# Reordering the last pair of quads in a Strassen-like QKV projection

## The chip, the cores and the metric

The kernel runs on one core of a Trainium2 chip. The metric is the device time of one execution in microseconds; the median of several runs is given. A core has a matrix engine (PE), a vector engine (VectorE, DVE in the profile), a scalar engine (ScalarE, ACT), GpSimd (POOL) and a queue engine (SyncE, SP) that here only issues transfers. All transfers of the core share 16 DMA engines.

## The reference

```python
x:     (16, 512, 768) float32      # 8192 rows of 768
w_qkv: (768, 2304)    float32
qkv = np.matmul(x, w_qkv)
q, k, v = qkv[..., :768], qkv[..., 768:1536], qkv[..., 1536:]
return np.stack([q, k, v], axis=0).astype(np.float32)     # (3, 16, 512, 768)
```

So it is one product of 8192x768 by 768x2304, whose columns are cut into three outputs.

## The kernel before

**Tiling.** The 8192 rows are taken as 32 pairs of 128-row tiles (`NP` = 32). The 2304 columns are two groups of 1024 (`q` = 0 and 1, at columns 0 and 1280) and a remainder of 256 columns between them (`REM`, at column 1024). One pair of row tiles by one column group is a *quad*: a 2x2 arrangement of output blocks c11, c12, c21 and c22, each 128x512, held in one SBUF tile `u.o`.

**Seven products.** A quad is not computed with eight block products but with seven, in the manner of Strassen-Winograd, out of sums of blocks of x (made by GpSimd in `sums_x`) and sums of blocks of w (made once by `sum_w`). `do(u, n)` issues product n (three matmuls of 128x128 by 128x512, in `product`, line 258) and the instruction that takes it out of PSUM. The products of a quad accumulate into three PSUM banks:

- bank `u.x`: product 1, read by ScalarE into c11 (`evacuate`, line 267); product 6 on top of it, read by ScalarE into c12 (line 286); product 7 on top of that, added by VectorE to c22 (line 295); product 4 on top of that, read by ScalarE into c21 (line 301).
- bank `u.y`: product 5, read by ScalarE into c22 (line 291, in the last pair of row tiles); product 3 on top of it, added by VectorE to c12 (line 304).
- bank `u.z`: product 2, added by VectorE to c11 (line 280).

So products 1, 6, 7 and 4 stand in a fixed order, and each of the last three can only start when the one before it has been read out of the bank; the same holds for 5 and 3. There are eight banks in all, handed out in turn by `bank()`.

**The remainder.** `rem_row(p, r, ps)` computes the 256 remaining columns of row tile r of pair p with six bf16 matmuls (line 321). In the last pair `rem_stored(p, r)` does this for one row tile, copies the result out of PSUM in two halves of 128 columns (ScalarE, line 423, and VectorE, line 424) and stores 128 KB from ScalarE's queue (line 426).

**Order.** The schedule is written by hand: each engine executes its instructions in the order in which the program issues them, and the framework only puts in semaphore waits where data or buffers demand it. Over the steady part of the kernel two quads of a pair run interleaved (`summed`, `plain`). The last pair of row tiles is done by `last(a, b)`, where a and b are its two quads. There each block is stored on its own as soon as it is complete (`store_cols`, 256 KB, line 416) from SyncE's queue, except one that goes from ScalarE's. After the last store has landed, the program closes (its waits stand under line 700).

Of the kernel before, what the change touches and what calls it, by code (L numbers as in the profile page):

```python
# [10 lines left out]
def kernel(  # L11
# [20 lines left out]
    nc = tc.nc  # L32
# [10 lines left out]
    CB = 512  # L43
    REM = N3 - 4 * CB
# [5 lines left out]
    ident = mybir.ActivationFunctionType.Identity  # L50
# [189 lines left out]
    def quad(p, q, pool=o_pool, tag="o"):  # L240
        u = Quad()
        u.p, u.q = p, q
        u.o = pool.tile([P, 2, 2 * CB], fp32, name="o", tag=tag)
        u.x = u.y = u.z = None
        return u

    def product(u, n, ps, start):
        t1, t2, t3, t4 = ts[u.q]
        if n <= 2:
            h = (n - 1) * KH  # L250
            lhs = [xb[u.p][:, h + j, :P] for j in range(KH)]
            rhs = [b1[u.q][:, h + j, :] for j in range(KH)]
        else:
            k, t = {3: (4, b22[u.q][:]), 4: (0, t4), 5: (1, t1), 6: (2, t2), 7: (3, t3)}[n]
            lhs = [sr[u.p][:, k, j, :] for j in range(KH)]
            rhs = [t[:, j, :] for j in range(KH)]
        for j in range(KH):
            nc.tensor.matmul(  # L258
                ps[:], lhs[j], rhs[j],
                start=(start and j == 0), stop=(j == KH - 1), skip_group_check=True,  # L260
            )

    def bank():
        return ps_pool.tile([P, CB], fp32, name="ps")

    def evacuate(u):
        nc.scalar.activation(u.o[:, 0, :CB], u.x[:], ident)

    def do(u, n, out=True):
        c11, c12 = u.o[:, 0, :CB], u.o[:, 0, CB:]  # L270
        c21, c22 = u.o[:, 1, :CB], u.o[:, 1, CB:]
        if n == 1:
            u.x = bank()
            product(u, 1, u.x, True)
            if out:
                evacuate(u)
        elif n == 2:
            u.z = bank()
            product(u, 2, u.z, True)
            nc.vector.tensor_tensor(c11, c11, u.z[:], op=add)  # L280
        elif n == 6:
            first = u.x is None
            if first:
                u.x = bank()
            product(u, 6, u.x, first)
            nc.scalar.activation(c12, u.x[:], ident)  # L286
        elif n == 5:
            u.y = bank()
            product(u, 5, u.y, True)
            if u.p == NP - 1:  # L290
                nc.scalar.activation(c22, u.y[:], ident)
        elif n == 7:
            product(u, 7, u.x, False)
            if u.p == NP - 1:
                nc.vector.tensor_tensor(c22, c22, u.x[:], op=add)
            else:
                nc.scalar.activation(c22, u.x[:], ident)  # L297
                nc.vector.tensor_tensor(c22, c22, u.y[:], op=add)  # L298
        elif n == 4:
            product(u, 4, u.x, False)  # L300
            nc.scalar.activation(c21, u.x[:], ident)  # L301
        elif n == 3:
            product(u, 3, u.y, False)
            nc.vector.tensor_tensor(c12, c12, u.y[:], op=add)  # L304
# [14 lines left out]
    def rem_row(p, r, ps):  # L319
        for j in range(KT):  # L320
            nc.tensor.matmul(  # L321
                ps, xb[p][:, j, r * P:(r + 1) * P], w_rem[j // KH][:, j % KH, :],
                start=(j == 0), stop=(j == KT - 1), skip_group_check=True,
            )
# [77 lines left out]
    def store_cols(u, r, lo, hi, eng):  # L402

        c = Q_OFF[u.q] + lo
        n = hi - lo
        row = (2 * u.p + r) * P
        src = u.o[:, r, lo:hi]
        left = (c // H + 1) * H - c
        if left >= n:
            dst = out_flat[c // H, row:row + P, c % H:c % H + n]  # L410
        else:
            assert 2 * left == n
            first = out_flat[c // H, row:row + P, c % H:H]
            dst = bass.AP(first.tensor, first.offset, [[H, P], [M * H - H + left, 2], [1, left]])
            src = src.rearrange("m (s n) -> m s n", s=2)
        eng.dma_start(dst, src)

    def rem_stored(p, r):
        ps = bank()
        rem_row(p, r, ps[:, :REM])  # L420
        o = or_pool.tile([P, 2, REM], fp32, name="orem")
        half = REM // 2
        nc.scalar.activation(o[:, 0, :half], ps[:, :half], ident)  # L423
        nc.vector.tensor_copy(out=o[:, 0, half:], in_=ps[:, half:REM])  # L424
        row = (2 * p + r) * P
        nc.scalar.dma_start(out_flat[1, row:row + P, R_OFF - H:R_OFF - H + REM], o[:, 0, :])

    def last(a, b):

        do(a, 1)  # L430
        do(b, 1)
        rem_stored(a.p, 0)
        for u in (a, b):
            do(u, 2)
            store_cols(u, 0, 0, CB, nc.sync)
        do(a, 6)
        do(b, 6)
        for u in (a, b):
            do(u, 5)
            do(u, 7)  # L440
            store_cols(u, 1, CB, 2 * CB, nc.sync)
        for u in (a, b):
            do(u, 4)
            store_cols(u, 1, 0, CB, nc.scalar if u is a else nc.sync)
            do(u, 3)
            store_cols(u, 0, CB, 2 * CB, nc.sync)
        rem_stored(a.p, 1)


# [130 lines left out]
    u = quad(2, 0)  # L580
# [72 lines left out]
    for p in range(ND + 3, NP - 1, 2):  # L653
# [14 lines left out]
        a, b = quad(p, 0), quad(p, 1)  # L668
# [3 lines left out]
        plain(a, b, c, d, early, lambda: rem(c.p)()(), final)  # L672
        summed(c, d, {} if final else {0: lambda: transpose(p + 3, 2, 0)}, "parts" if final else True)
    last(quad(NP - 1, 0), quad(NP - 1, 1))


# [28 lines left out]
```

## Time and profile before

| what | value |
|---|---|
| median of 3 runs | 359.17 us (358.98 to 359.32) |
| the profiled execution's own time | 358.81 us |
| span in its profile (first to last instruction) | 357.0 us |
| PE busy | 350.6 us, 98% of the span |
| VectorE, ScalarE, GpSimd busy | 264.4, 185.0, 177.3 us |
| granted clock of PE | 1.00 of full speed |
| last pair begins on PE at | 342.93 us |
| last matmul ends, last store is issued | 353.68, 354.35 us |

The execution's own time is 1.8 us longer than the span, which counts from the first to the last instruction of the program. Times in the views are microseconds from the span's start. In a line such as `352.36 0.60 ACT L301 ... x1 [0.76 <-PE ps L258]` the columns are the start, the length, the engine, the line of the kernel, the operation with its operands and shapes, the number of instructions, and in brackets how long the engine was idle before and which engine, tile and line ended that. PEld is the weight load of the matrix engine, which can overlap its matmuls; a matmul's length includes its way through the array, so that matmuls in a row start closer together than they are long.

### The profile page before, as it was taken

The numbers are of one execution on the slowest core, as the hardware profiler recorded it, in microseconds if no ns is written. First come the engines' busy times: TensorE is split into PE (matmuls) and PEld (weight loads), VectorE is DVE, ScalarE is ACT, GpSimd is POOL, SyncE is SP. The second block draws the span as 40 slices with busy tenths as digits, with TensorE's granted clock in tenths as the row PEclk, the third lists the DMA queues.
The fourth block names the chain that finished last, engine by engine and source line by source line (L and its number), as shares of the span: only waits on it lengthen the run. The fifth ranks groups of instructions, "written<-read, shape, count | busy, mean of one in ns | idle before, by whom it ended". The sixth has DMA issues, their size and how long they took to land.

```text
span 357.0 us, 5315 instructions
## 1 busy us (share of the span) xinstructions
PE 350.6 (98%) x1757; PEld 252.1 (71%) x1776; DVE 264.4 (74%) x310; ACT 185.0 (52%) x317; POOL 177.3 (50%) x184
## 2 busy tenths in 40 slices
PE   7999999999999999999999999999999999999996
PEld 3474677768677686877768677686877768677674
DVE  3789876796877869777695877869777695876743
ACT  4587754545454553645545454553645545454553
POOL 0031773376566453665535566353665535566320
PEclk9999999999999999999999999999999999999999
DMA  7997999999999898998979899698999979887497
GB/s 296 380 353 238 325 378 340 373 317 348 308 311 340 257 361 206 347 266 285 361 197 385 227 342 307 209 402 213 347 263 307 331 196 392 225 303 280 155 380 260
DMA packets 82075, 108.10 MB, mean 303 GB/s; under 512 B 4992, under 2 KB 62080, under 8 KB 82048
## 3 DMA queue, kind: packets, MB, share of 16 engines
q1 hardware_dynamic: 75088, 102.52, 85.7%
q10 hardware_dynamic: 6960, 5.24, 5.5%
q8 instruction: 14, 0.23, 0.3%
q14 instruction: 13, 0.11, 0.1%
HBM read 32.24 MB, written 75.50 MB: 302 GB/s over the span
## 4 chain that ended last, share of the span: by engine, by line
PE 74%; POOL 15%; DVE 6%; issue 3%; DMA 2%; ACT 0%; SPq 0%
PE ps L258 56%; PE ps L321 12%; PE ps L496 6%; DVE xf L155 6%; POOL xb L205 5%; POOL s L226 3%; POOL s L225 3%; POOL s L227 3%; DMA xin<-in_x_dram 2%; PE ps L185 0%; DVE o L304 0%; ACT xc L166 0%; SPq L162 0%; DVE orem L424 0%; ACT orem L423 0%
## 5 line engine op out<-in xcount | busy, mean ns | idle before, releaser
L258 PE MATMUL ps<-t,s 128*128 128x512 f32 x720 | 177.9, 395 | 0.0
L258 PEld LDWEIGHTS ps<-t,s 128*128 128x128 f32 x720 | 135.1, 188 | 29.5
L155 DVE STREAM_TRANSPOSE xf<-xin 128x768 f32<-128x768 f32 (+1 forms) x45 | 93.3, 2075 | 4.3 <-DMA xin<-in_x_dram 4.3
L258 PE MATMUL ps<-b,xb 128*128 128x512 bf16 x343 | 81.6, 379 | 1.1
L298 DVE TENSOR_TENSOR o<-o,ps 128x512 f32<-128x512 f32 x56 | 38.5, 688 | 50.7 <-ACT o L297 50.0
L205 POOL CAST xb<-xf 128x1536 bf16<-128x1536 f32 x28 | 41.1, 1467 | 56.9 <-DVE xf L155 54.8
L225 POOL TENSOR_TENSOR s<-xf 128x384 fp32r<-128x384 f32 x29 | 31.0, 1068 | 72.9 <-DVE xf L155 71.1
L258 PEld LDWEIGHTS <-xb 128*128 128x128 bf16 x360 | 33.9, 98 | 36.7 <-issue 3.9
L304 DVE TENSOR_TENSOR o<-o,ps 128x512 f32<-128x512 f32 x60 | 41.1, 687 | 20.5 <-PE ps L258 19.4
L297 ACT ACTIVATE o<-ps 128x512 f32<-128x512 f32 x56 | 33.5, 598 | 42.1 <-PE ps L258 42.1
L258 PE MATMUL ps<-b,s 128*128 128x512 f32 x180 | 50.6, 389 | 0.0
L301 ACT ACTIVATE o<-ps 128x512 f32<-128x512 f32 x60 | 35.9, 598 | 25.2 <-PE ps L258 22.8
L378 DVE TENSOR_TENSOR o<-o,ps 128x512 f32<-128x512 f32 x78 | 47.8, 680 | 0.0
L321 PE MATMUL ps<-w_rem,xb 128*128 128x256 bf16 x384 | 47.4, 273 | 0.0
L286 ACT ACTIVATE o<-ps 128x512 f32<-128x512 f32 x60 | 35.9, 599 | 19.4 <-PE ps L258 14.0
L321 PEld LDWEIGHTS <-xb 128*128 128x128 bf16 x384 | 37.3, 98 | 11.5 <-issue 0.5
L335 ACT ACTIVATE orem<-ps 128x512 f32<-128x512 f32 x31 | 18.5, 598 | 48.3 <-PE ps L321 34.0
L258 PEld LDWEIGHTS ps<-b,s 128*128 128x128 f32 x180 | 33.8, 188 | 7.0
L226 POOL TENSOR_TENSOR s<-s,xf 128x384 fp32r<-128x384 f32 x29 | 29.5, 1018 | 2.3
L227 POOL TENSOR_TENSOR s<-xf 128x384 fp32r<-128x384 f32 x29 | 29.4, 1015 | 0.0
L229 POOL TENSOR_TENSOR s<-xf,s 128x384 fp32r<-128x384 f32 x29 | 29.2, 1008 | 0.0
L382 ACT ACTIVATE o<-ps 128x512 f32<-128x512 f32 x26 | 15.5, 598 | 17.9 <-PE ps L258 17.3
(49 smaller groups left out, 161.2 us busy)
## 6 DMA issues: line engine op xcount, KB each, us to landing
out_dram<-o SPq DMA_DIRECT2D x60, 768.0 KB, 4.6
out_dram<-o SPq DMA_DIRECT2D x75, 256.0 KB, 3.8
xin<-in_x_dram SPq DMA_DIRECT2D x88, 192.0 KB, 5.6
out_dram<-orem SPq DMA_DIRECT2D x31, 256.0 KB, 2.2
xin<-in_x_dram ACTq DMA_DIRECT2D x24, 192.0 KB, 4.4
st<-in_w_qkv_dram SPq DMA_DIRECT2D x5, 768.0 KB, 7.9
xin<-in_x_dram SPq DMA_DIRECT2D x2, 768.0 KB, 4.9
st<-in_w_qkv_dram SPq DMA_DIRECT2D x6, 256.0 KB, 6.0
```

Source lines behind the costliest of these rows:

```text
L155: nc.vector.transpose(turned[:, g:g + n], rows[:, g:g + n])
L205: nc.gpsimd.tensor_copy(out=xb[p][:], in_=xf[p][:])
L225: 1: lambda g: g.tensor_tensor(s[:, 1], a21, a22, op=add),
L226: 2: lambda g: g.tensor_tensor(s[:, 2], s[:, 1], a11, op=sub),
L227: 3: lambda g: g.tensor_tensor(s[:, 3], a11, a21, op=sub),
L258: nc.tensor.matmul(ps[:], lhs[j], rhs[j], start=(start and j == 0), stop=(j == KH - 1), skip_group_check=True,)
L286: nc.scalar.activation(c12, u.x[:], ident)
L298: nc.vector.tensor_tensor(c22, c22, u.y[:], op=add)
L301: nc.scalar.activation(c21, u.x[:], ident)
L304: nc.vector.tensor_tensor(c12, c12, u.y[:], op=add)
L321: nc.tensor.matmul(ps, xb[p][:, j, r * P:(r + 1) * P], w_rem[j // KH][:, j % KH, :], start=(j == 0), stop=(j == KT - 1), skip_group_check= ...
L378: dve.tensor_tensor(c, c, u.z[:], op=add)
```

## The change

`last` runs the same products and remainders in another order, and `rem_stored` copies a remainder with one ScalarE instruction of 256 columns instead of two halves on two engines. In the new order the first remainder leaves its place behind product 1 of the second quad and stands behind the second quad's product 7. The first quad's products 7, 4 and 3 are issued before the second quad's 7, 4 and 3. Product 4's store of the first quad goes from SyncE's queue instead of ScalarE's.

```diff
         ps = bank()
         rem_row(p, r, ps[:, :REM])
         o = or_pool.tile([P, 2, REM], fp32, name="orem")
-        half = REM // 2
-        nc.scalar.activation(o[:, 0, :half], ps[:, :half], ident)
-        nc.vector.tensor_copy(out=o[:, 0, half:], in_=ps[:, half:REM])
+        nc.scalar.activation(o[:, 0, :], ps[:, :REM], ident)
         row = (2 * p + r) * P
         nc.scalar.dma_start(out_flat[1, row:row + P, R_OFF - H:R_OFF - H + REM], o[:, 0, :])

         do(a, 1)
         do(b, 1)
-        rem_stored(a.p, 0)
         for u in (a, b):
             do(u, 2)
             store_cols(u, 0, 0, CB, nc.sync)
-        do(a, 6)
-        do(b, 6)
-        for u in (a, b):
-            do(u, 5)
-            do(u, 7)
-            store_cols(u, 1, CB, 2 * CB, nc.sync)
-        for u in (a, b):
-            do(u, 4)
-            store_cols(u, 1, 0, CB, nc.scalar if u is a else nc.sync)
-            do(u, 3)
-            store_cols(u, 0, CB, 2 * CB, nc.sync)
+        for u, n in ((a, 6), (a, 5), (a, 7), (b, 6), (b, 5)):
+            do(u, n)
+        store_cols(a, 1, CB, 2 * CB, nc.sync)
+        do(a, 4)
+        store_cols(a, 1, 0, CB, nc.sync)
+        do(a, 3)
+        store_cols(a, 0, CB, 2 * CB, nc.sync)
+        do(b, 7)
+        store_cols(b, 1, CB, 2 * CB, nc.sync)
+        rem_stored(a.p, 0)
+        do(b, 4)
+        store_cols(b, 1, 0, CB, nc.sync)
+        do(b, 3)
+        store_cols(b, 0, CB, 2 * CB, nc.sync)
         rem_stored(a.p, 1)
```

The products of the last pair on PE, in order (1a is product 1 of the first quad, R0 the first remainder):

```
before: 1a 1b R0 2a 2b 6a 6b 5a 7a 5b 7b 4a 3a 4b 3b R1
after:  1a 1b 2a 2b 6a 5a 7a 6b 5b 4a 3a 7b R0 4b 3b R1
```

## The prediction, made before the changed kernel ran

> **What bounds the kernel now.** I read the chain of waits over the last 14 us first, because the change touches only the last pair of quads. Its columns are start, length and what ran.
>
> ```profile
> 343.00 1.24 PE ps L258 x5
> 344.24 0.66 PE ps L321 x6
> 344.90 8.11 PE ps L258 x36
> 353.01 0.69 PE ps L321 x6
> 353.69 0.02 issue
> 353.71 0.29 ACT orem L423
> 354.00 0.02 issue
> 354.02 0.29 DVE orem L424
> ```
>
> The matrix engine (PE) runs its products end to end without one wait; from 342.93 its row of work is the path. Then come the two half copies of the last remainder, the VectorE half strictly behind the ScalarE half, the store issued at 354.35, its landing, and the close of the program at 357.0. So there are two ways to move the end: a hole in PE's row (every ns of it counts), or a shorter way from PE's last matmul to the last landing.
>
> The second view is the timeline of the same stretch (start, length, engine, line, operation, operands; in brackets the idle time before it and what ended it). From it I take the unit prices.
>
> ```profile
> 350.39 0.69 DVE L295 TENSOR_TENSOR o<-o,ps 128x512 f32<-128x512 f32 x1 [0.67 <-PE ps L258]
> 350.80 0.84 PE L258 MATMUL ps<-b,s 128*128 128x512 f32 x3
> 351.26 0.64 PEld L258 LDWEIGHTS ps<-t,s 128*128 128x128 f32 x3
> 351.49 0.84 PE L258 MATMUL ps<-t,s 128*128 128x512 f32 x3
> 352.17 0.84 PE L258 MATMUL ps<-b,s 128*128 128x512 f32 x3
> 352.36 0.60 ACT L301 ACTIVATE o<-ps 128x512 f32<-128x512 f32 x1 [0.76 <-PE ps L258]
> 352.85 0.83 PE L321 MATMUL ps<-w_rem,xb 128*128 128x256 bf16 x6
> 353.05 0.69 DVE L304 TENSOR_TENSOR o<-o,ps 128x512 f32<-128x512 f32 x1 [0.67 <-PE ps L258]
> 353.71 0.28 ACT L423 ACTIVATE orem<-ps 128x128 f32<-128x128 f32 x1 [0.75 <-PE ps L321]
> 354.02 0.29 DVE L424 COPY orem<-ps 128x128 f32<-128x128 f32 x1 [0.29 <-ACT orem L423]
> 354.35 0.34 ACTq L426 DMA_DIRECT2D out_dram<-orem  x1
> ```
>
> Call the products 1a to 7a of the first quad and 1b to 7b of the second, R0 and R1 the remainders. The rows 351.49 (4b) and 352.17 (3b) give a pitch of 0.68 us a product. 4b starts at 351.49 and ScalarE reads its bank at 352.36: a product's bank is read by ScalarE 0.87 after its start, and free again 0.60 later, at +1.47. 7b stands two products ahead of 3a (350.80), so it starts at 349.44; VectorE's add reads it at 350.39, which is +0.95, and frees the bank 0.69 later, at +1.64. A remainder takes 0.66 of PE's row (the chain's second line).
>
> The third view is the table of windows (length, busy time of each engine, granted clock, DMA share, GB/s).
>
> ```profile
> 349.50:351.90 2.40, 2.40 (x12) 2.01 (x11) 1.12 (x3) 1.20 (x2) 0.00 (x0) 1.00 0.39 137
> 351.90:355.50 3.60, 1.78 (x11) 1.07 (x10) 1.45 (x3) 0.87 (x2) 0.00 (x0) 1.00 1.02 378
> ```
>
> The DMA engines first lie mostly idle, then are full to the end: five stores of 256 KB and one of 128 KB come within 4 us.
>
> **The change part by part.** Orders on PE, before and after:
> before: 1a 1b R0 2a 2b 6a 6b 5a 7a 5b 7b 4a 3a 4b 3b R1
> after: 1a 1b 2a 2b 6a 5a 7a 6b 5b 4a 3a 7b R0 4b 3b R1
> The work of PE is the same. What matters is the distance between products on one bank: 1, 6, 7 and 4 of a quad accumulate into bank x, and each must wait until the product before it has been read out; 5 and 3 share bank y.
>
> *Distances that stay harmless.* 1a to 6a: 1b, 2a, 2b lie between, 6a is due 2.7 after 1a and the bank is free at 1.47. 7a to 4a: 6b and 5b lie between, due 2.04, free 1.64, as before. 6b to 7b, 5a to 3a and 5b to 3b have three products or more between. R0 takes a fresh bank. Cost 0, covered by those products; without them each would cost what the next two cost.
>
> *6a to 7a.* Before, 6b and 5a lay between (due 2.04); now only 5a does, so 7a is due at 2 x 0.68 = 1.36, while ScalarE has read 6a only at 1.47. A hole of 0.11 plus the restart r of PE after a release.
>
> *7b to 4b.* Before, 4a and 3a lay between; now R0 does: 4b is due at 0.68 + 0.66 = 1.34, and VectorE's add ends at 1.64. A hole of 0.30 plus r. VectorE is free in time: an add without a second wait starts 0.88 after its product (352.17 to 353.05), so 3a's, one product earlier, ends at 0.88 - 0.68 + 0.69 = 0.89 after 7b's start, ahead of the 0.95.
>
> *The restart r.* After the ramp the kernel shows no hole on PE, so r is bounded by rows of the start-up and of the steady stream. There PE waited for a ScalarE cast:
>
> ```profile
> 6.93 0.52 ACT L166 ACTIVATE xc<-xin 128x384 bf16<-128x384 f32 x1 [1.02 <-DMA xin<-in_x_dram]
> 7.51 0.67 PE L185 MATMUL ps<-eye,xc 128*128 128x128 bf16 x7 [0.58 <-ACT xc L166]
> ```
>
> The cast ended at 7.45, PE's first matmul stands at 7.51: r = 0.06, with bf16 weights. In the stream an f32 weight load at 351.26 precedes its matmul at 351.49 by 0.23; with the 0.06 and a separate wait of PE's sequencer (0.05 in the view of line 258) r is 0.34 at most. I take 0.17, nearer the low end, since in the stream most of the 0.23 is the load standing behind a running matmul, but an f32 load (0.19) is longer than a bf16 one (0.10). The holes are then 0.28 and 0.47, together 0.75; with r = 0.06, 0.53; with r = 0.34, 1.09. [...]
>
> *Who is queued behind.* While PE waits for 4b, 3b and R1 stand behind it, and so does everything to the end: the holes are paid in full.
>
> *The tail.* One ScalarE copy of 128x256 replaces two half copies in a row. ScalarE takes 0.28 for 128 columns and 0.60 for 512, so 256 cost 0.28 + 0.32/3 = 0.39. Before, the copies ended at 354.31, 0.60 after 353.71; now at 0.39: the last store is issued 0.22 earlier behind R1. It landed 1.8 us after issue (the view of line 426). From below: 3b's store (issued 353.76, landed 2.1 later) and R1's share the DMA engines, 128 KB at 378 GB/s are 0.35 us, and if R1's data queue behind 3b's the 0.22 is lost: gain 0. From above: the stores ahead are thinned (R0's 128 KB stands where a 256 KB store stood, and the hole before 4b adds a pause), so both may land with no queue; then 3b's store, landing 2.0 after issue (the least in the view of line 416), is the floor, R1's landing at 0.42 earlier. I take 0.22.
>
> *Moves without a price.* 4a's store goes from ScalarE's queue to SP's: SP's issues take 0.34 to 0.6 each and its stores become ready 0.6 or more apart. R0's copy (0.39) and its store's issue (0.38) now stand on ScalarE's queue behind 4a's read and ahead of 4b's; a remainder is read 0.86 after its start (352.85 to 353.71), so R0's copy runs from 0.68 + 0.86 = 1.54 to 1.93 after 7b's start and the issue ends near 2.35; 4b starts at 1.34 + 0.47 = 1.81 and is read at 2.68: covered by 4b itself. VectorE loses its half copies and the 1.59 it waited for the first; nothing waited for that.
>
> *Sum.* +0.75 - 0.22 = +0.53 on the profiled execution: 358.81 becomes 359.34, its span 357.0 becomes 357.5. That execution stands 0.36 under the median of 359.17, which becomes 359.70. The bounds are 0.53 - 0.42 = +0.11 and 1.09 - 0 = +1.09. A measurement of this kernel can tell about 0.2%, 0.72 us, from no change.
>
> **Rivals.**
> *The holes are dear (slower).* Place: 7a and 4b. If r is near 0.3 on f32 weights and the DMA queue swallows the tail's 0.22, the sum is 0.41 + 0.60 - 0.1 = +0.9: 360.1. With my tail it decides from r = 0.27 on. For it: f32 loads are twice as long as the row behind 0.06. Against it: that row.
> *No hole (a gain).* If the weights for 7a and 4b are ready and releases arrive earlier than the readers' rows say, only the tail is left: -0.22, 358.95; over 0.72 of gain would need more than the 0.42 the tail has. Against it: the order on PE is the written one, and the readers' lengths are fixed within 0.01.
> [...]
>
> **How the numbers follow.** The forecast of two holes of moderate size has 0.60, dear holes 0.30, no hole 0.05, the clock 0.02, and 0.03 is left for a gain over 0.2%. So faster 0.03, same 0.65, slower 0.32. The forecast's own range is 359.3 to 359.9; with the dear holes it reaches 360.4, and with no hole down to 359.0.
>
> **What would show it.** Right: PE idle of about 0.3 ahead of 7a, ended by ScalarE's L286, and about 0.45 ahead of 4b, ended by VectorE's L295; R1 starting near 353.6; a single L422 copy near 0.39; the close 4.6 us after 3b's start (now 4.83). Wrong: PE's row unbroken, or holes over 0.5 each; the last landing still tied to 3b's; a granted clock under 1.00 before the end.

## The result and the profile after

The changed kernel takes 359.76 us (median of 11 runs, 359.65 to 360.33) against 359.00 us before: a ratio of 1.0021, 95% interval 1.0013 to 1.0029. That is 0.75 us more (0.5 to 1.0), slower, and just on the bound that the prediction gave for what a measurement can tell ("about 0.2%, 0.72 us"). The profiled execution took 359.65 us, with a span of 357.9 against 357.0.

The chain that ended last, in order of time, in the changed kernel (start, length, what ran):

```profile
346.96 0.09 issue
347.05 3.68 PE ps L258 x15
350.73 0.02 issue
350.75 0.69 DVE o L304
351.44 0.01 DVEq L295
351.46 0.04 issue
351.50 0.70 DVE o L295
352.20 0.04 issue
352.25 1.66 PE ps L258 x6
353.91 0.68 PE ps L321 x6
354.59 0.02 issue
354.61 0.38 ACT orem L422
```

Before, this was one unbroken row of PE. Now it breaks twice. At 346.96 PE waits before 7a, and from 350.75 to 352.25 the chain leaves PE: it runs through VectorE's adds of 3a (line 304) and 7b (line 295), and PE only comes back when the second has freed bank x of the second quad. The add of 3a stands in the chain because 7b's add follows it on VectorE without a pause, but it did not hold 7b's add up: that began 0.94 after 7b's start, and 0.95 after it in the kernel before, where VectorE had stood idle for 0.67. The timeline has the same two places, with the idle time and its releaser in brackets (rows chosen from the stretch):

```profile
346.30 0.60 ACT L286 ACTIVATE o<-ps 128x512 f32<-128x512 f32 x1 [1.35 <-PE ps L258]
347.02 2.60 PEld L258 LDWEIGHTS ps<-t,s 128*128 128x128 f32 x12 [0.50 <-issue]
350.56 0.84 PE L258 MATMUL ps<-t,s 128*128 128x512 f32 x3
351.24 0.83 PE L321 MATMUL ps<-w_rem,xb 128*128 128x256 bf16 x6
351.50 0.69 DVE L295 TENSOR_TENSOR o<-o,ps 128x512 f32<-128x512 f32 x1
352.25 0.53 PEld L258 LDWEIGHTS ps<-t,s 128*128 128x128 f32 x3 [0.46 <-DVE o L295]
352.25 0.97 PE L258 MATMUL ps<-t,s 128*128 128x512 f32 x3 [0.18 <-DVE o L295]
353.05 0.86 PE L258 MATMUL ps<-b,s 128*128 128x512 f32 x3
354.61 0.38 ACT L422 ACTIVATE orem<-ps 128x256 f32<-128x256 f32 x1 [0.77 <-PE ps L321]
355.03 0.37 ACTq L424 DMA_DIRECT2D out_dram<-orem  x1
```

How to read a hole here: PE's bracket shows only 0.18 us, because a matmul's row (0.39 to 0.40 us in the stream) is longer than the distance to the next one's start (0.227), so that the row before a hole still covers part of the idle time. The true size is in the starts of single matmuls: the last of 5a, the second of 7a, the last of R0 and the second of 4b.

```profile
346.56 0.40 PE L258 MATMUL ps<-t,s 128*128 128x512 f32 x1
347.35 0.39 PE L258 MATMUL ps<-t,s 128*128 128x512 f32 x1
351.80 0.27 PE L321 MATMUL ps<-w_rem,xb 128*128 128x256 bf16 x1
352.58 0.40 PE L258 MATMUL ps<-t,s 128*128 128x512 f32 x1
```

The first two start 0.79 apart, and two pitches of the stream (the distance between the starts of matmuls in a row, 0.227) are 0.45: a hole of 0.34. The other two start 0.787 apart, where without a hole (in the kernel "fillboth" below) it is 0.344: a hole of 0.44.

The windows of the changed kernel around its holes and its tail (length, busy time of the engines, clock, DMA share, GB/s):

```profile
350.50:351.50 1.00, 1.00 (x7) 0.64 (x7) 0.69 (x1) 0.17 (x1) 0.00 (x0) 1.00 0.06 20
351.50:354.20 2.70, 2.52 (x17) 1.72 (x15) 0.94 (x2) 0.98 (x2) 0.00 (x0) 1.00 0.92 340
354.20:354.70 0.50, 0.38 (x4) 0.10 (x1) 0.43 (x1) 0.09 (x1) 0.00 (x0) 1.00 0.00 0
354.70:356.70 2.00, 0.00 (x0) 0.00 (x0) 0.00 (x0) 0.30 (x1) 0.00 (x0) 1.00 0.90 328
```

The queue of stores did empty ahead of the last ones (no byte moved from 354.2 to 354.7), as the prediction had it; but after it, from 354.7 to 356.7, the DMA engines are 0.90 busy again.

For the comparison with the experiments below, every time in this table is counted from the start of the last matmul ahead of the pair (342.54 in the profile before, 342.57 after), since the executions differ by up to 0.7 us in what comes earlier. The starts and landings are read from each kernel's trace; the ratio is of the time to the time of the kernel before.

| kernel | 3b starts | last store issued | 3b's store landed | last store landed | end | ratio (95% interval) |
|---|---|---|---|---|---|---|
| before | 9.62 | 11.80 | 13.30 | 13.64 | 14.47 | 1 |
| changed | 10.48 | 12.46 | 14.12 | 14.45 | 15.29 | 1.0021 (1.0013 to 1.0029) |
| fill7 | 10.18 | 12.15 | 13.81 | 14.14 | 14.98 | 1.0013 (1.0004 to 1.0022) |
| fill4 | 10.03 | 12.01 | 13.72 | 14.07 | 14.97 | 1.0013 (1.0004 to 1.0021) |
| fillboth | 9.71 | 11.69 | 13.39 | 13.72 | 14.62 | 1.0001 (0.9992 to 1.0010) |
| copyonly | 9.62 | 11.58 | 13.29 | 13.64 | 14.47 | 1.0000 (0.9991 to 1.0009) |
| split | 10.48 | 12.68 | 14.11 | 14.44 | 15.28 | 1.0023 (1.0014 to 1.0032) |
| no3b | 9.62 | 11.58 | none | 13.26 | 14.16 | 0.9992 (0.9983 to 1.0001) |
| r0end | 9.00 | 11.86 | 12.68 | 13.56 | 14.40 | 0.9998 (0.9989 to 1.0006) |
| r0endsp | 9.00 | 11.62 | 12.70 | 13.36 | 14.33 | 0.9994 (0.9985 to 1.0003) |

By this count the changed kernel ends 0.82 us later: 3b starts 0.86 later, and the way from 3b's start to the end is 4.81 instead of 4.85.

The last two columns do not always lie equally far apart. When the last store has landed, SyncE still has to find that out: at the close it checks the semaphores of the stores one after the other, in the order of its instructions (in the kernel before the last three of these rows stand at 355.22, 355.86 and 356.20, each 0.02 behind a landing). In six of the ten kernels the last store is checked last, one check follows its landing, and the end comes 0.84 after it. In fill4, fillboth and no3b two checks follow it and the end comes 0.90 after it; in r0endsp three, and 0.97. So a difference of 0.06 between two ends can be one check more, and the landings are the cleaner measure of the stores.

### The profile page after: what moved, and what is told of

It reads as the page before. It is cut to its first block, busy times and chain, and to the rows that moved or that the text cites. A ratio compares the mean times of both kernels' runs of the same rounds, so it can differ in the third digit from the quotient of the medians.

```text
span 357.9 us, 5332 instructions
## 1 busy us (share of the span) xinstructions
PE 352.6 (99%) x1776; PEld 252.0 (70%) x1776; DVE 263.2 (74%) x308; ACT 185.5 (52%) x317; POOL 177.8 (50%) x184
## 4 chain that ended last, share of the span: by engine, by line
PE 97%; DMA 2%; DVE 0%; ACT 0%; SPq 0%; issue 0%; DVEq 0%
PE ps L258 79%; PE ps L321 12%; PE ps L496 6%; DMA xin<-in_x_dram 2%; PE ps L185 0%; DVE o L295 0%; DVE o L304 0%; ACT xc L166 0%; SPq L162 0%; ACT orem L422 0%; DVEq L295 0%
## 5 line engine op out<-in xcount | busy, mean ns | idle before, releaser
L258 PE MATMUL ps<-b,xb 128*128 128x512 bf16 x360 | 85.2, 379 | 0.0
L225 POOL TENSOR_TENSOR s<-xf 128x384 fp32r<-128x384 f32 x29 | 29.5, 1017 | 72.3 <-DVE xf L155 70.6
L227 POOL TENSOR_TENSOR s<-xf 128x384 fp32r<-128x384 f32 x29 | 29.5, 1016 | 0.0
```

What stands on the lines that cost most here:

```text
L225: 1: lambda g: g.tensor_tensor(s[:, 1], a21, a22, op=add),
L258: nc.tensor.matmul(ps[:], lhs[j], rhs[j], start=(start and j == 0), stop=(j == KH - 1), skip_group_check=True,)
```

## The experiments

Theory one: the time is in the two holes. Its first rival: they only move idle time about, and the loss is in the new order of the stores or the copy. A second question is why the single copy gave nothing: whether the last landing follows its issue, or 3b's store. In the excerpts of code, some lines are left out (...), and loops are written out where a line moves.

**fill7**: one product moved into the first hole.

```diff
-        do(b, 2)
-        store_cols(b, 0, 0, CB, nc.sync)
         do(a, 6)
         do(a, 5)
+        do(b, 2)
+        store_cols(b, 0, 0, CB, nc.sync)
         do(a, 7)
```

> The changed kernel with 2b moved to between 5a and 7a, so that 7a is due 2.04 us after 6a's start again. Theory one (the time is in the two holes of the matrix engine, 0.34 ahead of 7a and 0.44 ahead of 4b): the first hole goes, 4b's stays at 0.44; 3b starts about 0.34 earlier than in the changed kernel (near 352.7 us), span near 357.5, time about 0.4 us over the kernel before. Rival (the loss sits in the new order of stores and in the single copy, and the holes only move idle time that was there): span stays near 357.9, 0.75 us over the kernel before.

Its chain:

```profile
344.92 5.71 PE ps L258 x25
...
351.40 0.70 DVE o L295
352.10 0.04 issue
352.14 1.67 PE ps L258 x6
```

The break before 7a is gone (PE runs from 344.92 through it), the one before 4b is as it was. 3b starts 0.31 earlier than in the changed kernel and the end comes 0.31 earlier: the hole of 0.34, less 0.03. The time agrees at 1.0013, 0.5 us over the kernel before, though its interval overlaps that of the changed kernel; the trace carries the verdict.

**fill4**: one product moved into the second hole.

```diff
-        do(a, 3)
-        store_cols(a, 0, CB, 2 * CB, nc.sync)
         do(b, 7)
+        do(a, 3)
         store_cols(b, 1, CB, 2 * CB, nc.sync)
+        store_cols(a, 0, CB, 2 * CB, nc.sync)
         rem_stored(a.p, 0)
```

> The changed kernel with 3a moved to between 7b and the first remainder, so that 4b is due about 2.0 us after 7b's start again. Theory one: 4b's hole of 0.44 goes, 7a's stays at 0.34; 3b starts near 352.6 us, span near 357.4, time about 0.35 us over the kernel before. Rival (stores and copy): span near 357.9.

Its chain:

```profile
347.29 0.09 issue
347.38 4.34 PE ps L258 x18
351.73 0.67 PE ps L321 x6
352.40 1.40 PE ps L258 x6
```

Now the wait before 7a is alone; from R0 (351.73) to 4b there is none, and VectorE is no longer in the chain. 3b starts 0.46 earlier, as much as the hole; the end only 0.32 earlier, since the tail is 0.13 longer again (4.94 from 3b's start to the end, against 4.81). Of that, 0.06 is the second check at the close. The other 0.07 lies ahead of the last landing, in the stores: 4b's and 3b's are issued 0.65 apart instead of 0.79, and 3b's takes 2.08 to land instead of 2.03. That the closer issues are the reason was not tried separately.

**fillboth**: both moves.

> Both moves together on the changed kernel. Theory one: no hole, 3b starts within 0.1 us of the kernel before (352.2 us); the tail after 3b is 0.0 to 0.1 us shorter than before, so span 356.9 to 357.1 and a time within 0.2 us of the kernel before. If the landing of the last store follows its issue by a fixed 1.8 us: 0.2 us faster than the kernel before, span 356.8. Rival (stores and copy): 0.5 us or more over the kernel before.

```profile
344.81 6.38 PE ps L258 x28
351.19 0.67 PE ps L321 x6
351.86 1.40 PE ps L258 x6
353.25 0.68 PE ps L321 x6
```

The chain is PE alone again, and the time is that of the kernel before (1.0001). So the two holes carry the loss, and the rival falls: it asked for 0.5 us or more here. The trace still ends 0.15 later than before, where 0.0 to 0.1 earlier was expected: 3b starts 0.09 late without any hole, and the tail is 0.06 longer. The 0.06 is the second check at the close: from 3b's start to the last landing it is 4.01, as in the kernel before. The order without its holes brings nothing.

**copyonly**: the kernel before with the single copy.

```diff
-        half = REM // 2
-        nc.scalar.activation(o[:, 0, :half], ps[:, :half], ident)
-        nc.vector.tensor_copy(out=o[:, 0, half:], in_=ps[:, half:REM])
+        nc.scalar.activation(o[:, 0, :], ps[:, :REM], ident)
```

> The kernel before with only the single ScalarE copy of 256 columns in place of the two halves. Theory one (the last store's data stand behind the store of 3b in the DMA engines): the last store is issued 0.22 us earlier but lands 0 to 0.06 us earlier, 0.33 to 0.35 us behind 3b's as before; span 356.9 to 357.0, no change in time. Rival (landing follows issue by a fixed 1.8 us): it lands 0.22 us earlier, span 356.8.

Its timeline and then the waits of SyncE's queue at the end (who waited for what: sum, times, longest; line 698 is the close of the program here):

```profile
354.32 0.38 ACT L422 ACTIVATE orem<-ps 128x256 f32<-128x256 f32 x1 [0.75 <-PE ps L321]
354.37 0.34 SPq L416 DMA_DIRECT2D out_dram<-o  x1
354.74 0.34 ACTq L424 DMA_DIRECT2D out_dram<-orem  x1
```

```profile
SPq L698 <- DMA out_dram<-o: 1.6, 3, 0.6
SPq L698 <- DMA out_dram<-orem: 0.3, 1, 0.3
```

The store is issued 0.37 behind 3b's store, where it had been 0.59; that is the 0.22 that the copy saves. It lands at 13.64, to the hundredth where it landed before: its way from issue to landing went from 1.83 to 2.05. In both kernels it lands 0.34 behind 3b's store, the 0.3 in the second line of the waits, and 128 KB at 395 GB/s, which the DMA engines moved from 354.5 to 355.5 in the kernel before, are 0.33 us.

**split**: the changed kernel with the two half copies put back (the edit above, reversed).

> The changed kernel's order with the two half copies put back (only the copy undone). Theory (the copy is worth nothing because the last landing is tied to 3b's): holes as in the changed kernel, the last store issued 0.22 us later, landing within 0.06 us of the changed kernel's, counted from the last pair's start; time 0.6 to 0.9 us over the kernel before. Rival (landing follows issue): 0.2 us later than the changed kernel, about 1.0 us over the kernel before.

```profile
355.16 0.29 DVE L424 COPY orem<-ps 128x128 f32<-128x128 f32 x1 [0.29 <-ACT orem L423]
355.48 0.37 ACTq L426 DMA_DIRECT2D out_dram<-orem  x1
```

The issue is 0.22 later than in the changed kernel (12.68 against 12.46), the landing the same (14.44 against 14.45), the time 1.0023. In neither order does the saving at issue reach the landing.

**no3b**: copyonly, with the store of 3b left out.

```diff
             do(u, 3)
-            store_cols(u, 0, CB, 2 * CB, nc.sync)
+            if u is a:
+                store_cols(u, 0, CB, 2 * CB, nc.sync)
```

> The kernel before with the single copy, and without the last store of 3b (256 KB of the output are not written). Queue theory: the last store's latency falls from 2.05 us to 1.6 to 1.85 us, the end comes 0.2 to 0.45 us earlier. Rival (fixed latency): still 2.0 us, end as before.

```profile
SPq L699 <- DMA out_dram<-orem: 0.6, 1, 0.6
```

Issued at the same 11.58, the last store now lands at 13.26 instead of 13.64, 1.68 after its issue, and the end comes 0.31 earlier (0.37 less the second check at the close). So 0.37 of the 2.05 us in copyonly go with 3b's store; I read them as a wait behind its data.

**r0end**: the single copy, the order of before, and both remainders last.

```diff
         do(b, 1)
-        rem_stored(a.p, 0)
...
             store_cols(u, 0, CB, 2 * CB, nc.sync)
+        rem_stored(a.p, 0)
         rem_stored(a.p, 1)
```

(4a's store goes from SyncE's queue here, as in the changed kernel; the lines above do not show it.)

> Single copy, the order of the kernel before, but with the first remainder between 3b and the second remainder: 6b 5a 7a 5b 7b 4a 3a 4b 3b R0 R1, so that no bank is revisited early and the store of 3b is issued 0.66 us further ahead of the last one. Queue theory (the last store's 128 KB wait behind 3b's store in the DMA engines, 0.33 to 0.35 us behind its landing in all runs so far): no hole, the second remainder starts where it does before, the last store is issued 0.22 us earlier and lands within 1.6 to 1.85 us instead of 2.0 to 2.05, more than 0.5 us behind 3b's landing; end 0.2 to 0.45 us earlier than before, counted from the last pair's start. Rival (the 2.0 us are the price of a store issued behind a 256-column copy, whatever else is under way): latency stays at 2.0 to 2.05, end as before.

```profile
353.02 0.38 ACT L422 ACTIVATE orem<-ps 128x256 f32<-128x256 f32 x1 [0.75 <-PE ps L321]
353.43 0.38 ACTq L424 DMA_DIRECT2D out_dram<-orem  x1
353.91 0.38 ACT L422 ACTIVATE orem<-ps 128x256 f32<-128x256 f32 x1 [0.51 <-PE ps L321]
354.32 0.37 ACTq L424 DMA_DIRECT2D out_dram<-orem  x1
```

The latency did fall, to 1.71, 0.88 behind 3b's landing. But the end is only 0.07 earlier: ScalarE was issuing R0's store until 353.81, and R1's copy, which could have begun when PE ended at 353.63, began at 353.91. The step that I had not priced is that issue on the copying engine.

**r0endsp**: the same, with R0's store on SyncE's queue.

```diff
-        rem_stored(a.p, 0)
+        rem_stored(a.p, 0, nc.sync)
```

> The same as the kernel with both remainders last, but the first remainder's store goes from SyncE's queue. There its issue on ScalarE (0.38 us) held up the copy of the second remainder by 0.25 us. Queue theory: the copy starts 0.03 us after PE's last matmul ends, the last store is issued about 0.25 us earlier, lands 1.65 to 1.85 us later, and the end comes 0.2 to 0.3 us earlier than with ScalarE's queue, 0.25 to 0.4 us earlier than the kernel before; time 0.05 to 0.15% under it, at the edge of what five rounds tell. Rival (the first remainder's 128 KB, landing near the same time, take the place of 3b's store as the one to wait for): issue earlier, landing unchanged, end 0.07 us earlier than before.

```profile
353.18 0.38 ACT L422 ACTIVATE orem<-ps 128x256 f32<-128x256 f32 x1 [0.75 <-PE ps L321]
353.66 0.41 SPq L424 DMA_DIRECT2D out_dram<-orem  x1
353.83 0.38 ACT L422 ACTIVATE orem<-ps 128x256 f32<-128x256 f32 x1 [0.27 <-PE ps L321]
354.24 0.38 ACTq L424 DMA_DIRECT2D out_dram<-orem  x1
```

The copy now follows PE's last matmul at once (353.83, 0.04 after its row ends) and the issue is 0.24 earlier. The last landing is 0.20 earlier than r0end's, 1.75 after its issue and 0.27 earlier than before, as the queue theory asked. The end is only 0.07 earlier than r0end's and 0.15 earlier than before, half of what I expected or less: the last store is now the first of three that SyncE checks at the close, and 0.13 goes there (0.97 from the last landing to the end, against 0.84). The rival, that R0's store takes the place of 3b's, asked for an unchanged landing and falls for the most part: R1 does land 0.33 behind R0's store (13.36 and 13.04), but its way from issue to landing is only 0.04 longer than in r0end. Among the kernels that write the whole output this is the best by trace and by ratio, but 0.9994 with an interval up to 1.0003 is not a gain that these runs can tell.

## Why the prediction was right, and which term was not

The mechanism was right: two holes at the two forecast places, ended by the two forecast readers, carry the loss. That the forecast of 359.70 us lies so near the measured 359.76 is luck. The sum was +0.53 on the profiled execution, and the profiled executions differ by 0.84 (358.81 and 359.65): 0.31 too little. To that the forecast added 0.36, the distance of the median from the profiled execution before, known from three runs; in the changed kernel it is 0.11: 0.25 too much. Between the medians of eleven runs the change is +0.76.

- *6a to 7a.* Predicted 0.11 + 0.17 = 0.28, measured 0.34. ScalarE had read the bank at 346.90, and 7a would have been due at 346.79 (5a's last start, 346.56, and a pitch): 0.11, as computed. The restart was 0.23, not 0.17; PE's sequencer had a wait of its own here (0.05, from 346.94) in front of the weight load at 347.02.
- *7b to 4b.* Predicted 0.30 + 0.17 = 0.47, measured 0.44. VectorE's add began 0.94 after 7b's start (350.56 to 351.50) and ended at 352.19, 0.30 after 4b would have been due. The rest of the 0.44 is the restart, 0.14. Both restarts lie between the bounds of 0.06 and 0.34. The row of 4b's first matmul stands at 352.25, 0.06 behind the add, as in the start-up row that gave the lower bound; so the distance from a release to a row's start is less than what PE loses. 4b's first load and first matmul stand at the same 352.25, the load lasts 0.19, and the second matmul starts 0.34 after the first's row, so that by an estimate the first streamed from about 0.11 on (0.34 less a pitch of 0.23), ahead of the load's end.
- *The harmless distances* were harmless: fillboth, which keeps most of them, has a chain of PE alone, and 7a to 4a shows no wait after the change. (1a to 6a took 2.6 and not 2.7: the bf16 matmuls of products 1 and 2 follow each other at 0.216.)
- *The queues.* R0's copy and issue on ScalarE (352.10 to 352.90) ended before 4b's read at 353.25, as computed.
- *The tail* is the term that failed: "I take 0.22". From 3b's start to the end the changed kernel takes 4.81 against 4.85, so 0.04. The lower bound in the prediction's own words, "if R1's data queue behind 3b's the 0.22 is lost", is what happens: copyonly and split show the saving of 0.22 at issue and none at landing, and no3b shows 0.37 of waiting that goes with 3b's store. The pause that empties the queue earlier is worth the 0.04 and no more: 3b's store comes after it, lands 2.03 after its issue instead of 2.09, and is issued 0.37 ahead of the last one, which still lands 0.33 behind it. Two of the prediction's own signs came out accordingly: the end 4.81 after 3b's start and not 4.6, and "the last landing still tied to 3b's", which it had listed under wrong.
- *Not in the sum.* 3b starts 0.86 late, and the holes are 0.78 of it. The other 0.08 appears mostly as f32 matmuls of the quads that follow each other at 0.23 or more instead of 0.227: 11 of 24 pitches in the changed kernel, 2 of 28 before; what they exceed 0.227 by adds up to 0.07, against 0.01 before. fillboth has 10 of 24 without holes. With the measured holes, tail and this the sum is 0.78 - 0.04 + 0.08 = 0.82.
- *The rivals.* "The holes are dear" had its size from r near 0.3 and a swallowed tail: the second half was true, the first not. Its +0.9 lies nearer to the 0.82 of the traces than the forecast's +0.53. "No hole" is refuted by the chain. For a fall of the clock, which the chances give 0.02, no run has a sign: with holes of 0.34 and 0.44 the granted clock stayed at 1.00 in every window across them and to the last store's landing, and its mean over any one run was 0.998 or more.

The chances put 0.65 on a change within 0.2% and 0.32 on a slower one; the measured ratio lies on the line between, and with the tail at 0.04 in place of 0.22 the forecast sum would have been +0.71, on that line too.

What stays open: why the quads' matmuls run mostly at 0.230 to 0.236 us for 0.9 to 1.7 us after a change of operand type or a break, and at 0.227 later. The rows show neither a granted clock under 1.00 nor one other engine that is busy in all of these stretches. The DMA engines are full or nearly so there (share 1.03, 1.06 and 0.93 in the three stretches of the changed kernel, 1.06 in the one of the kernel before), but so they are from 347 to 349 in the kernel before (1.07), at 0.227. It was not tried separately.

## What to carry to other kernels

Where products accumulate on one PSUM bank and are read out in between, list for every bank the time from a product's start until its reader has freed it (here 1.47 us with a ScalarE copy, 1.64 with a VectorE add), and compare it with the work that the new order puts in between. A product too few cost the difference plus 0.14 to 0.23 us of restart here, and the order that spreads the stores better did not pay for it. A shorter last copy was worth nothing here, where the DMA engines were still full (share 0.98 from the last store's issue at 354.35 to 355.85 in the kernel before). So look at the gap between the last two landings first; where it was the last store's bytes over the bandwidth (0.34 us, and 128 KB at 395 GB/s are 0.33), an earlier issue gained nothing. What moving bytes ahead is worth was not shown: leaving 3b's bytes out brought the end 0.31 us earlier, moving the remainders brought 0.07 and 0.15 by trace and nothing that the times can tell. Look also at who issues the store: in r0end ScalarE issued one for 0.38 us, and the last copy, due on ScalarE meanwhile, began 0.25 us late. And count the checks at the close that follow the last landing: each was 0.06 to 0.07 us.

## What was not expected of the hardware

- The last landing moved by less than 0.01 us when its store was issued 0.22 earlier (copyonly against the kernel before, the changed kernel against split): up to that point the issue had slack.
- The last store's 128 KB took 1.68 us from issue to landing with 3b's store left out (no3b), and 1.76 to 2.06 with that store's 256 KB issued 0.37 to 0.59 ahead.
- The end came 0.84, 0.90 or 0.97 us after the last landing, with one, two or three of SyncE's checks still to come (r0end, fillboth, r0endsp).
- Matmuls of 128x512 with f32 operands ran mostly at a pitch of 0.230 to 0.236 us after each break or change of type, against 0.227 in the stream, with the granted clock at 1.00.
